# The output product `w_o` of a macaron block as two pairs of Strassen groups, with weight forms prepared early and kept in DRAM

## The chip, the cores and the metric

The kernel runs on one core of one Trainium2 chip. The metric is the device time of one execution in microseconds (us); lower is better. The kernel before takes 2166.26 us, the median of three runs (2164.23 to 2166.77).

Names used below: PE is TensorE (matrix products), DVE is VectorE, ACT is ScalarE, SP is SyncE, whose queue issues nearly all DMA transfers in this kernel. SBUF is the on-chip memory that the engines read, PSUM the accumulators that PE writes, DRAM the memory of the device outside the core.

## What is computed

One layer of a streaming encoder on 1024 tokens of width 1024, all in float32. Cut to what matters:

```python
h = x + 0.5 * swiglu(rmsnorm(x), ffn1_w_in, ffn1_w_out)     # width 2816 inside
u = rmsnorm(h)
q, k, v, g_ret, p, gates = split(u @ w_in)
ret  = retention(rotary(q), rotary(k), v); ret = headnorm(ret) * silu(g_ret)
pool = multiscale_pool(p)
gate = sigmoid(gates + gate_bias)
merged = gate[0] * (ret @ w_ret_up) + gate[1] * (pool @ w_pool_up)
h = h + merged @ w_out                                      # the product that the change is about
h = h + 0.5 * swiglu(rmsnorm(h), ffn2_w_in, ffn2_w_out)
out = rmsnorm(h)
```

`w_out` is 1024 x 1024 and is called `w_o` in the kernel.

## The kernel before

**Layout.** Activations are kept transposed: a tile is 128 channels by 1024 tokens, so 1024 channels are 8 tiles `mt` = 0 to 7, and each tile has two halves `j` of 512 tokens. A matmul takes a 128x128 block of weights and 128x512 of an operand.

**Precision.** Each float32 operand is split into two parts: `hi`, a cast on ACT (`copy`, L152), and `lo`, the remainder by one subtraction on DVE (L153; L156 and L157 where a gain is multiplied in). A product is three matmuls, hi x hi, hi x lo, lo x hi (`mm3`, L172 to L174; L612 to L615 in `plain`).

**Strassen groups.** Most large products go through `strassen`. A group is two output tiles, `i` and `i+4`, by two token halves: a 2x2 block product in seven block products instead of eight (the Winograd variant). Two groups make a pair, which shares weights. The seven products of a pair use seven forms of the weights (L11, S2, S1, S3, L12, S4, L22, made from four blocks by additions, then split) and seven forms of the operand (R11, T2, T1, T3, R21, R22, T4), four k-tiles each. The class `Next` makes the forms of an operand as its quadrants (tile, half) become ready: `r11`, `t2` (two operations on DVE and a split), `t1`, `t3`, `r21`, `p22`, `t4_`. `in_turn` puts pairs in sequence; `first`, `middle` and `final` give the order of the seven products (numbers 0 to 6 stand for the forms in the order listed), and `apart` runs that many of the last products group by group rather than alternating. Groups hand their output quadrants to an `evac` function, in the order in which products finish.

**`plain`** is the other kind of product: one output tile at a time, 8 k-tiles, no Strassen. The pooling projection (`pu`) and `w_o` go this way.

**Order of the work.** `Flow.run` lays out the instructions: it takes steps, each with a preparation and a body of matmuls; a preparation is emitted `LOOK` = 4 steps before its body. Small work (gating, operand forms, statistics) goes into a queue, `flow.add`, from which `flow.rate` items are emitted after each body; `flow.until` empties the queue up to what a body needs. A scheduler then sets the order on each engine: instructions that are ready go in the order in which they were emitted, and those inside `soon()` go first. It also gives out buffers: each tag has a fixed number, and an instruction that writes a new tile waits until one is free. The tags that matter here: `raw` (5 of 128x1024: weight blocks before their split), `wt` (3 of twice that: split weights), `tl` (3), `t4` (9), `mv` (28 split operands), `c2` (6), and PSUM's 6 banks and 2 for sums. Each engine, and SP's queue of transfers, executes its instructions in order.

**The stages around the change.** The first feed-forward's down-projection is `ffn_out` (names beginning with `b`): products p1 and p6 alternating, p2 and p7 alternating, then p5, p3, p4, each 11 steps `k` of 12 matmuls. Its weights come in blocks through `raw` (names `bL`), two `k` at a time; p5 and p3 read weights that are already in SBUF. Then follow the projections `w_in` (Strassen pairs, the first is `q0`, `k0`), the values (`values`, `w_v`, seven products p1, p2, p6, p5, p3, p7, p4 of two steps each), the retention with the pooling matmuls and `pu` as fillers, and `merge`.

`merge` (from L1583 on) first multiplies by `w_ret` in two Strassen pairs with operand `up` (28 `mv` tiles, all in use at the start of its second pair). The groups are `ru0` to `ru3`: `group(i)` evacuates quadrants into tiles `ru{i}A` and `ru{i}B` and, when a group is complete, loads its gate tiles (`rgt` into `tl`) and pooling tiles (`rpm` into `raw`), multiplies and adds them half by half (L1562, L1563), and splits each half into an operand `mg` (4 per group, 16 in all). Then `w_o` runs as eight `plain` products over these in the order 0, 4, 1, 5, 2, 6, 3, 7; each loads a 512 KB block `wo{mt}raw` and splits it (`wo{mt}w`); its evacuation adds the residual `h1` (L1592) and feeds `ffn2`, the `Next` of the second feed-forward (names `n3`), whose first product writes `c_a`.

Of the kernel before, what the change touches and what calls it, by code (L numbers as in the profile page):

```python
# [17 lines left out]
P = 128  # L18
S = 1024
# [73 lines left out]
def block_kernel(ctx: ExitStack, tc, x, x_tok, vecs, f1_in, f1_out, w_in, w_v, pool_w, w_ret, w_pool, w_o,  # L93
# [45 lines left out]
    def load(dst, src):  # L139
        nc.sync.dma_start(dst, src)  # L140
# [4 lines left out]
    def half(t, j):  # L145
        return t[:, j * H : (j + 1) * H]
# [23 lines left out]
    def mm3(dst, w, m, start, stop):  # L170

        mm(dst, w[0], m[0], start=start, stop=False, skip_group_check=True)  # L172
        mm(dst, w[0], m[1], start=False, stop=False, skip_group_check=True)  # L173
        mm(dst, w[1], m[0], start=False, stop=stop, skip_group_check=True)  # L174

    def parts(m, at=slice(None)):
        return m[:, 0, at], m[:, 1, at]
# [226 lines left out]
    def none():  # L404
        pass

    def strassen(nx, src, outs, order, inner=False):

# [35 lines left out]

        def prep(n, make=None):
            def go():
                if make:
                    make()
                if n == "S2":
                    s2()  # L450
                t["w", n] = weights(t[n], f"{tag}w{n}")

            return go

        def prod(z, dst, w, m, start, stop):
            for i in range(4):
                mm3(G[z][dst], parts(t["w", w], 4 * z + i), parts(nx.operand(m, i)), start and i == 0, stop and i == 3)

        def u(z, n):
            G[z][n] = c2(f"{outs[z][0]}{n}")  # L460
# [103 lines left out]
            return [(none if z else f, lambda z=z: body(z)) for z in range(len(outs))]  # L564

        def first_prep():
            blocks()
            t["w", "L11"] = weights(t["L11"], f"{tag}wL11")

# [153 lines left out]
    ops_done = {}  # L723


    def ffn_out(ops, ready, w, res, name, sink, end, final=None):

# [278 lines left out]
    def ffn1():  # L1006
        for n, step in enumerate(ffn_in(first, f1_in, ops1, "a", lead)):
            flow.rate = 1 if n < 40 else 2
            yield step
        yield from ffn_out(ops1, ops_done["a"], f1_out, x, "b", mix.quarter, end1)  # L1010

    mix = Next("n2", V_MIX, h1)

# [122 lines left out]
    def values(order, inner):  # L1136
# [74 lines left out]
        def u1(t):  # L1211
            copy(of("U1", t), b["a"][t])
# [116 lines left out]
    class Unit:  # L1329
# [137 lines left out]
        def finish(self, last=False):  # L1467
            for i in range(2):
# [11 lines left out]
                else:  # L1480
                    load(ret[2 * self.h + i], g)

    units = [Unit(h, nh) for h in range(NH) for nh in range(2)]
    up = Next("ru", V_ONE, within=0)

# [51 lines left out]
        yield from fill(2 * KT)  # L1537


    MG = {}  # L1540

    def group(i):
        pair = []
        name = f"ru{i}"

        def evac(which, in0, in1):
            if not pair:
                pair.extend((t4(f"{name}A"), t4(f"{name}B")))
            tile, j = which
            dst = half(pair[tile], j)  # L1550
            if in1 is None:
                copy(dst, in0)
            else:
                tt(dst, in0, in1, ADD)

        def gate(z):
            mt, t = i + 4 * z, pair[z]
            g, o = tl(f"rgt{mt}"), raw(f"rpm{mt}")
            load(g, gates[mt])
            load(o, pm[mt])  # L1560
            for j in range(2):
                flow.add(lambda j=j: tt(half(t, j), half(t, j), half(g, j), MUL),  # L1562
                         lambda j=j: tt(half(t, j), half(t, j), half(o, j), ADD))  # L1563

            def put():
                MG[mt] = [operand(half(t, j), f"mg{mt}{j}") for j in range(2)]

            flow.add(put)

        def end():  # L1570
            for z in range(2):
                gate(z)

        return name, evac, end

    PAIRED = (0, 4, 1, 5, 2, 6, 3, 7)

    def merged(n):
        mt = PAIRED[n]
        flow.until(lambda: mt in MG)  # L1580
        return MG[mt]

    def merge():  # L1583
        yield from in_turn(up, (lambda *how, n=n: strassen(up, [w_ret[n, k] for k in range(4)], [group(2 * n), group(2 * n + 1)], *how)
                                for n in range(2)), middle=(0, 3, 1, 4, 2, 6, 5), final=(0, 3, 1, 4, 2, 6, 5), apart=2)
        for mt in PAIRED:

            def evac(dst, mt=mt):
                base, h = tl(f"h1_{mt}"), t4(f"h2_{mt}")
                load(base, h1[mt])  # L1590
                for j in range(2):
                    tt(half(h, j), dst[j], half(base, j), ADD)  # L1592
                for j in range(2):
                    flow.add(lambda j=j: ffn2.quarter(mt, slice(j * H, (j + 1) * H), half(h, j)))
                i = mt - 4
                if i >= 0:
                    flow.add(lambda: ffn2.r11(i), lambda: ffn2.r22(i), lambda: ffn2.t2(i),
                             lambda: ffn2.t1(i))
                if mt == 7:
                    ffn2.work(ffn2.t3)  # L1600
                    ffn2.stats()
                    ffn2.work(ffn2.r21, ffn2.p22, ffn2.t4_)
# [140 lines left out]
def lay_out(i):  # L1743
# [19 lines left out]
    def halves(w):  # L1763
# [21 lines left out]
        "w_o": tiles(i["w_out"][0]).reshape(KT, P, 2, 4, P).transpose(0, 1, 3, 2, 4).reshape(KT, P, D),  # L1785
# [25 lines left out]
```

## Time and profile before

| | |
|---|---|
| median of three runs | 2166.26 us |
| profiled execution, its own time | 2167.76 us |
| span of the profiled execution | 2166.0 us |
| PE busy | 2152.6 us, 10432 matmuls |
| DVE busy | 1699.7 us, 2388 instructions |
| ACT busy | 990.5 us, 1553 instructions |
| DMA, mean over the span | 146 GB/s, 316.63 MB |
| granted clock of PE | 0.999 of full speed |

The profile is of one execution; its span goes from the first to the last recorded instruction, and 1.76 us of the execution's time lie outside it. Busy time of an engine is the time in which it executes an instruction; in the views below, each row of a timeline gives start and length in us, engine, source line, operation, output and inputs by their names in the program, shapes, and in brackets the idle time before it with what ended it. A row of groups gives busy time in us, mean length in ns and idle time before. Buffer numbers are left out of names.

### The profile page before, as it was taken

How to read it: one execution, taken by the hardware profiler on the slowest of the kernel's cores; microseconds unless marked ns; L12 is line 12 of the kernel's file. 1: busy time of each engine (PE TensorE's matmuls, PEld its weight loads, DVE VectorE, ACT ScalarE, POOL GpSimd, SP SyncE). 2: the span in 40 equal slices, each digit the busy share in tenths (PEclk: the TensorE clock that was granted, in tenths of full speed). 3: DMA queues.
4: the chain of work that ended last, by engine and by line, in shares of the span. 5: the costliest groups of instructions: out<-in, count | busy, mean ns of one | idle time of the engine just before them, and what ended most of it. 6: DMA issues, size and time to landing. Idle time of an engine off the chain costs nothing.

```text
span 2166.0 us, 27380 instructions
## 1 busy us (share of the span) xinstructions
PE 2152.6 (99%) x10432; PEld 1816.6 (84%) x10432; DVE 1699.7 (78%) x2388; ACT 990.5 (46%) x1553; POOL 0.2 (0%) x4
## 2 busy tenths in 40 slices
PE   9999999999999999999999999999999999999998
PEld 7888888888888888888888998878888888888887
DVE  8698687898789888978777676866887868788875
ACT  7534343445544443434344765443533334344453
POOL 0000000000000000000000000000000000000000
PEclk9999999999999999999999999999999999999999
DMA  5343323496333332333375565463232322348622
GB/s 205 115 151 115 105 93 118 153 328 227 123 99 112 108 125 98 127 108 107 125 249 198 174 215 205 134 208 117 78 117 93 119 101 98 120 157 316 231 95 83
DMA packets 117500, 316.63 MB, mean 146 GB/s; under 512 B 12380, under 2 KB 18936, under 8 KB 117368
## 3 DMA queue, kind: packets, MB, share of 16 engines
q1 hardware_dynamic: 116824, 314.36, 42.6%
q8 instruction: 82, 1.34, 0.3%
q10 hardware_dynamic: 544, 0.52, 0.1%
q14 instruction: 50, 0.41, 0.1%
HBM read 225.17 MB, written 89.67 MB: 145 GB/s over the span
## 4 chain that ended last, share of the span: by engine, by line
PE 94%; DVE 3%; DMA 2%; ACT 1%; issue 0%; SPq 0%; ACTq 0%; DVEq 0%
PE c_b L172 2%; PE c_b L173 2%; PE c_b L174 2%; PE a_b L172 2%; PE a_b L174 2%; PE a_b L173 2%; PE c_e L172 2%; PE c_a L172 2%; PE c_e L173 2%; PE c_a L173 2%; PE c_e L174 2%; PE c_a L174 2%; PE a_e L172 2%; PE a_e L173 2%; PE a_e L174 2%; PE a_a L174 2%
## 5 line engine op out<-in xcount | busy, mean ns | idle before, releaser
L172 PE MATMUL c_a<-n3R,c_wL 128*128 128x512 f32 x176 | 68.6, 390 | 0.0
L173 PE MATMUL c_a<-n3R,c_wL 128*128 128x512 f32 x176 | 68.5, 389 | 0.0
L173 PE MATMUL c_b<-n3T,c_wS 128*128 128x512 f32 x176 | 68.5, 389 | 0.0
L174 PE MATMUL c_a<-n3R,c_wL 128*128 128x512 f32 x176 | 68.5, 389 | 0.0
L174 PE MATMUL c_b<-n3T,c_wS 128*128 128x512 f32 x176 | 68.5, 389 | 0.0
L172 PE MATMUL c_b<-n3T,c_wS 128*128 128x512 f32 x176 | 68.5, 389 | 0.0
L172 PE MATMUL a_b<-n1T,a_wS 128*128 128x512 f32 x168 | 65.5, 390 | 0.6 <-ACT a_b L469 0.6
L172 PE MATMUL a_a<-n1R,a_wL 128*128 128x512 f32 x168 | 65.5, 390 | 0.0
L174 PE MATMUL a_b<-n1T,a_wS 128*128 128x512 f32 x168 | 65.4, 389 | 0.0
L173 PE MATMUL a_a<-n1R,a_wL 128*128 128x512 f32 x168 | 65.4, 389 | 0.0
L174 PE MATMUL a_a<-n1R,a_wL 128*128 128x512 f32 x168 | 65.4, 389 | 0.0
L173 PE MATMUL a_b<-n1T,a_wS 128*128 128x512 f32 x168 | 65.4, 389 | 0.0
L152 ACT CAST c_wL<-c_L 128x1024 fp32r<-128x1024 f32 x33 | 34.5, 1050 | 64.5 <-PE c_b L174 49.1
L153 DVE TENSOR_TENSOR c_wS<-c_L,c_wS 128x1024 fp32r<-128x1024 f32 x33 | 40.4, 1223 | 26.3 <-ACT c_wS L152 26.2
L152 ACT CAST a_wL<-a_L 128x1024 fp32r<-128x1024 f32 (+1 forms) x33 | 33.4, 1011 | 53.1 <-PE a_b L174 44.0
L153 DVE TENSOR_TENSOR a_wS<-a_L,a_wS 128x1024 fp32r<-128x1024 f32 (+1 forms) x33 | 38.7, 1173 | 23.2 <-ACT a_wS L152 22.0
L153 DVE TENSOR_TENSOR a_wL<-a_L,a_wL 128x1024 fp32r<-128x1024 f32 (+1 forms) x33 | 38.7, 1172 | 8.6 <-ACT a_wL L152 8.6
L153 DVE TENSOR_TENSOR c_wL<-c_L,c_wL 128x1024 fp32r<-128x1024 f32 x33 | 40.2, 1221 | 4.6 <-ACT c_wL L152 4.5
L152 ACT CAST c_wS<-c_L 128x1024 fp32r<-128x1024 f32 x33 | 34.6, 1052 | 10.1 <-PE wo3d L615 3.5
L174 PEld LDWEIGHTS c_b<-n3T,c_wS 128*128 128x128 f32 x176 | 33.0, 188 | 6.9
L174 PEld LDWEIGHTS c_a<-n3R,c_wL 128*128 128x128 f32 x176 | 33.0, 188 | 6.9
L173 PEld LDWEIGHTS c_b<-n3T,c_wS 128*128 128x128 f32 x176 | 33.0, 188 | 6.9
(2648 smaller groups left out, 7461.3 us busy)
## 6 DMA issues: line engine op xcount, KB each, us to landing
c_L<-in_f_in SPq DMA_DIRECT2D x44, 512.0 KB, 3.5
a_L<-in_f_in SPq DMA_DIRECT2D x40, 512.0 KB, 3.5
bL<-in_f_out SPq DMA_DIRECT2D x25, 512.0 KB, 4.7
dL<-in_f_out SPq DMA_DIRECT2D x20, 512.0 KB, 5.4
v<-in_w_v SPq DMA_DIRECT2D x16, 512.0 KB, 4.3
t<-au SPq DMA_DIRECT2D x11, 512.0 KB, 4.2
b<-an SPq DMA_DIRECT2D x11, 512.0 KB, 2.6
r<-au SPq DMA_DIRECT2D x11, 512.0 KB, 3.6
```

The lines of the kernel that those rows point to most:

```text
L152: copy(hi, src)
L153: tt(lo, src, hi.bitcast(F32), SUB)
L172: mm(dst, w[0], m[0], start=start, stop=False, skip_group_check=True)
L173: mm(dst, w[0], m[1], start=False, stop=False, skip_group_check=True)
L174: mm(dst, w[1], m[0], start=False, stop=stop, skip_group_check=True)
```

## The change

`w_o` is computed as two Strassen pairs with a `Next` called `mg` as operand: each quadrant of `merged` is gated as it is evacuated (its gate and pooling halves are loaded one quadrant ahead, into `tl`), and the seven forms of `mg` are made by group. The outputs are evacuated by quadrant, onto the residual. `PAIRED`, `merged`, `MG` and the use of `plain` for `w_o` go.

The seven weight forms of each pair don't depend on activations. They are made earlier, by `out_weights`: each form is loaded, added up, split into `hi` and `lo`, and both parts are stored to DRAM (`o_forms`, 1 MB a form). Ten of the fourteen are put into the flow beside steps of p5 (k = 0, 2, 4, 6, 8, 10) and p3 (k = 1, 3, 5, 7) of the first down-projection, four after the values' p3. `strassen` gets a parameter `ready`: with it, the preparation of a product only loads its form, into two `raw` tiles for the forms named in `ready` (L11 and L12 of the first pair), into one `wt` tile for the others.

```diff
+BESIDE = [('p5', k) for k in (0, 2, 4, 6, 8, 10)] + [('p3', k) for k in (1, 3, 5, 7)]
...
-    def strassen(nx, src, outs, order, inner=False):
+    def strassen(nx, src, outs, order, inner=False, ready=None):
...
         def prep(n, make=None):
             def go():
+                if ready is not None:
+                    if n in ready:
+                        two = [sb.tile([P, S], F32R, tag="raw", bufs=N_RAW, name=f"{tag}w{n}{j}") for j in range(2)]
+                        t["w", n] = two
+                        for j in range(2):
+                            load(two[j].bitcast(F32), src[n][:, j].rearrange("p a b -> p (a b)"))
+                        return
+                    t["w", n] = wt(f"{tag}w{n}")
+                    load(t["w", n].bitcast(F32), src[n])
+                    return
...
+                if (n, k) in BESIDE:
+                    flow.add(*(f for _, f in zip(range(1), beside)))
...
                 if (o, j) == (0, 1):
-                    flow.add(pools[1][0], pools[2][0])
+                    flow.add(pools[1][0], pools[2][0], *forms_of_o)
...
+    o_forms = [{n: dr.tile([P, 2, 8, P], F32, tag=f"of{k}{n}", name=f"of{k}{n}")
+                for n in ("L11", "S2", "S1", "S3", "L12", "S4", "L22")} for k in range(2)]
+
+    def out_weights(k):
+        t = {}
+        def block(n):
+            r = raw(f"o{k}{n}_{len(t)}")
+            t[len(t)] = r
+            load(r, w_o[k, n])
+            return r
+        def keep(n, r):
+            hi = sb.tile([P, S], F32R, tag="raw", bufs=N_RAW, name=f"oh{k}{n}")
+            lo = r
+            if n in ("S1", "S2"):
+                lo = raw(f"ol{k}{n}")
+            copy(hi, r)
+            tt(lo.bitcast(F32R), r, hi.bitcast(F32), SUB)
+            for j, v in enumerate((hi.bitcast(F32), lo)):
+                load(o_forms[k][n][:, j].rearrange("p a b -> p (a b)"), v)
+        def s1():
+            t["S"] = block(1)
+            tt(t["S"], t["S"], block(2), ADD)
+            keep("S1", t["S"])
...
+        return l11, l12, s3, s1, s2, s4, l22
+    forms_of_o = chain(out_weights(0), out_weights(1))
...
-    MG = {}
+    mg = Next("mg", V_ONE, within=0)
...
+        order = [(1, 1), (0, 0), (0, 1), (1, 0)] if i < 2 else [(0, 0), (1, 1), (1, 0), (0, 1)]
+        def gate(which):
+            z, j = which
+            mt = i + 4 * z
+            g = G[which] = tl(f"rg{mt}{j}")
+            load(half(g, 0), half(gates[mt], j))
+            load(half(g, 1), half(pm[mt], j))
...
             if in1 is None:
-                copy(dst, in0)
+                tt(dst, in0, half(g, 0), MUL)
             else:
                 tt(dst, in0, in1, ADD)
+                flow.add(lambda: tt(dst, dst, half(g, 0), MUL))
+            flow.add(lambda: tt(dst, dst, half(g, 1), ADD))
+            done.append(which)
+            forms = {(0, 0): [mg.r11], (1, 1): [mg.p22], (1, 0): [mg.r21]}.get(which, [])
+            if which != (1, 0) and len({(0, 0), (0, 1), (1, 1)}.intersection(done)) == 3:
+                forms += [mg.t2, mg.t3, mg.t1]
+            if len(done) == 4:
+                forms += [mg.t4_]
+            flow.add(*(lambda f=f: f(i) for f in forms))
...
+        def begun():
+            if not pair:
+                pair.extend(t4(f"{name}{z}") for z in range(2))
+                for z in range(2):
+                    load(pair[z], h1[i + 4 * z])
+        def evac(which, in0, in1):
+            begun()
+            z, j = which
+            mt, dst = i + 4 * z, half(pair[z], j)
+            tt(dst, in0, dst, ADD)
+            if in1 is not None:
+                flow.add(lambda: tt(dst, dst, in1, ADD))
+            flow.add(lambda: ffn2.quarter(mt, slice(j * H, (j + 1) * H), dst))
...
     def merge():
+        flow.rate = 4
...
-            yield from plain(merged, KT, w_o[mt], f"wo{mt}", evac)
+        yield from in_turn(mg, (lambda *how, n=n: strassen(mg, o_forms[n], [output(2 * n), output(2 * n + 1)], *how, ready=({'L11', 'L12'}, ())[n])
+                                for n in range(2)), first=(0, 4, 3, 1, 2, 6, 5), final=(0, 4, 3, 1, 2, 5, 6), apart=0)
```

On the host, `w_o` is laid out in the four blocks of each pair, as `w_ret` is.

More of the change, by code (lines that the diff above doesn't have):

```diff
@@ L456, in prod @@
             for i in range(4):
-                mm3(G[z][dst], parts(t["w", w], 4 * z + i), parts(nx.operand(m, i)), start and i == 0, stop and i == 3)
+                k = 4 * z + i
+                two = t["w", w]
+                two = [v[:, k * P : (k + 1) * P] for v in two] if isinstance(two, list) else parts(two, k)
+                mm3(G[z][dst], two, parts(nx.operand(m, i)), start and i == 0, stop and i == 3)
         def u(z, n):
@@ L566, in first_prep @@
         def first_prep():
+            if ready is not None:
+                return prep("L11")()
             blocks()
@@ L723, in block_kernel, with ffn_out @@
     ops_done = {}
-    def ffn_out(ops, ready, w, res, name, sink, end, final=None):
+    def ffn_out(ops, ready, w, res, name, sink, end, final=None, beside=iter(())):
         R, T, B, T4 = ops
@@ L1009, in ffn1 @@
             yield step
-        yield from ffn_out(ops1, ops_done["a"], f1_out, x, "b", mix.quarter, end1)
+        yield from ffn_out(ops1, ops_done["a"], f1_out, x, "b", mix.quarter, end1,
+                           beside=forms_of_o)
     mix = Next("n2", V_MIX, h1)
@@ L1481, in finish, with l11, s2, s4 @@
                     load(ret[2 * self.h + i], g)
+    o_forms = [{n: dr.tile([P, 2, 8, P], F32, tag=f"of{k}{n}", name=f"of{k}{n}")
[16 more added lines that the diff above has]
+                load(o_forms[k][n][:, j].rearrange("p a b -> p (a b)"), v)
+        def l11():
+            keep("L11", block(0))
+        def s1():
+            t["S"] = block(1)
+            tt(t["S"], t["S"], block(2), ADD)
+            keep("S1", t["S"])
+        def s2():
+            tt(t["S"], t["S"], block(0), SUB)
+            keep("S2", t["S"])
+        def s4():
+            tt(t["S"], block(3), t["S"], SUB)
+            keep("S4", t["S"])
+        def s3():
+            r = block(0)
+            tt(r, r, block(1), SUB)
+            keep("S3", r)
+        def l12():
+            keep("L12", block(3))
+        def l22():
+            keep("L22", block(2))
+        return l11, l12, s3, s1, s2, s4, l22
+    forms_of_o = chain(out_weights(0), out_weights(1))
     units = [Unit(h, nh) for h in range(NH) for nh in range(2)]
@@ L1548, in evac @@
                 pair.extend((t4(f"{name}A"), t4(f"{name}B")))
-            tile, j = which
-            dst = half(pair[tile], j)
+                gate(which)
+            n = order.index(which)
+            if n < 3:
+                gate(order[n + 1])
+            z, j = which
+            dst, g = half(pair[z], j), G[which]
+            mg.tiles[i + 4 * z, j] = dst
             if in1 is None:
-                copy(dst, in0)
+                tt(dst, in0, half(g, 0), MUL)
             else:
                 tt(dst, in0, in1, ADD)
[L1556 to L1568, printed above, removed]
+                flow.add(lambda: tt(dst, dst, half(g, 0), MUL))
@@ new lines, in evac, with output @@
+            flow.add(lambda: tt(dst, dst, half(g, 1), ADD))
[6 more added lines that the diff above has]
+            flow.add(*(lambda f=f: f(i) for f in forms))
+        return name, evac, none
+    def output(i):
+        pair = []
+        name = f"wo{i}"
+        def begun():
[5 more added lines that the diff above has]
+            begun()
+            z, j = which
+            mt, dst = i + 4 * z, half(pair[z], j)
[3 more added lines that the diff above has]
+            flow.add(lambda: ffn2.quarter(mt, slice(j * H, (j + 1) * H), dst))
+            if (z, j) == (0, 0):
+                flow.add(lambda: ffn2.r11(i))
+            if (z, j) == (1, 1):
+                flow.add(lambda: ffn2.r22(i))
+            if (z, j) == (0, 1):
+                flow.add(lambda: ffn2.t2(i), lambda: ffn2.t1(i))
@@ L1570, in end @@
         def end():
-            for z in range(2):
-                gate(z)
+            if i == 3:
+                ffn2.work(ffn2.t3)
+                ffn2.stats()
+                ffn2.work(ffn2.r21, ffn2.p22, ffn2.t4_)
         return name, evac, end
[L1576 to L1581, printed above, removed]
     def merge():
+        flow.rate = 4
         yield from in_turn(up, (lambda *how, n=n: strassen(up, [w_ret[n, k] for k in range(4)], [group(2 * n), group(2 * n + 1)], *how)
@@ L1585, in merge @@
                                 for n in range(2)), middle=(0, 3, 1, 4, 2, 6, 5), final=(0, 3, 1, 4, 2, 6, 5), apart=2)
[L1586 to L1602, printed above, removed]
-            yield from plain(merged, KT, w_o[mt], f"wo{mt}", evac)
+        yield from in_turn(mg, (lambda *how, n=n: strassen(mg, o_forms[n], [output(2 * n), output(2 * n + 1)], *how, ready=({'L11', 'L12'}, ())[n])
+                                for n in range(2)), first=(0, 4, 3, 1, 2, 6, 5), final=(0, 4, 3, 1, 2, 5, 6), apart=0)
@@ L1784, in lay_out @@
         "w_pool": tiles(i["w_pool_up"][0]),
-        "w_o": tiles(i["w_out"][0]).reshape(KT, P, 2, 4, P).transpose(0, 1, 3, 2, 4).reshape(KT, P, D),
+        "w_o": quads(i["w_out"][0], [(n, n + 4) for n in range(4)]),
         "f2_in": quads(i["ffn2_w_in"][0], swiglu(SWIGLU)),
```

2 lines of the change are left out of this document (1 added, 1 removed).

## The prediction

> **What bounds the kernel now.** I read the page's busy times and its chain of work first, then the waits of TensorE, then busy times by stage (the windows view), and last the timelines of TensorE, VectorE and SyncE at the places that the change touches.
>
> ```profile
> span 2166.0 us, 27380 instructions
> ...
> PE 2152.6 (99%) x10432; PEld 1816.6 (84%) x10432; DVE 1699.7 (78%) x2388; ACT 990.5 (46%) x1553; POOL 0.2 (0%) x4
> ...
> PE 94%; DVE 3%; DMA 2%; ACT 1%; issue 0%; SPq 0%; ACTq 0%; DVEq 0%
> ```
>
> TensorE (PE) is busy for 2152.6 of 2166.0 us and carries 94% of the chain that ended last. Time can therefore go in two ways only: fewer matmuls, or fewer stalls of PE; and it can come back in one, as a new stall. The windows view (per row: length, then busy time and instructions of PE, PEld, DVE, ACT, POOL, then granted clock, DMA share, GB/s) shows the stages in question: two for the product before `w_o` (its first and second pair), `w_o` itself, the three last steps of the first down-projection (p5, p3, p4), and the end of the values.
>
> ```profile
> 1361.20:1399.40 38.20, 38.20 (x170) 31.65 (x169) 29.66 (x37) 14.87 (x21) 0.00 (x0) 1.00 0.46 142
> 1399.40:1437.50 38.10, 38.10 (x169) 31.55 (x169) 28.57 (x39) 19.21 (x29) 0.00 (x0) 1.00 0.60 189
> 1437.50:1526.20 88.70, 88.07 (x385) 71.84 (x385) 53.26 (x73) 26.61 (x40) 0.00 (x0) 1.00 0.41 143
> 548.90:578.80 29.90, 29.90 (x133) 24.76 (x132) 23.84 (x34) 17.32 (x26) 0.00 (x0) 1.00 0.43 138
> 578.80:608.80 30.00, 30.00 (x133) 24.68 (x132) 13.36 (x18) 11.99 (x17) 0.00 (x0) 1.00 0.12 44
> 608.80:638.70 29.90, 29.90 (x133) 24.75 (x133) 29.68 (x42) 15.37 (x24) 0.00 (x0) 1.00 0.33 104
> 1148.30:1170.00 21.70, 21.70 (x97) 18.00 (x96) 9.47 (x13) 3.35 (x4) 0.00 (x0) 1.00 0.59 191
> ```
>
> PE is full in every one of them but the `w_o` stage, the clock is granted in full, and VectorE (DVE) is the next engine: nearly full in p4, a quarter idle in the pair before `w_o`.
>
> **The matmuls removed.** First starts in PE's timeline give the period and the length of the stage; the groups by line give the count.
>
> ```profile
> 1399.46 0.39 PE L172 MATMUL ru2a<-ruR,ru2wL 128*128 128x512 f32 x1
> ...
> 1437.54 0.39 PE L612 MATMUL wo0d<-mg,wo0w 128*128 128x512 f32 x1
> ...
> 1526.22 0.39 PE L172 MATMUL c_a<-n3R,c_wL 128*128 128x512 f32 x1
> ```
>
> ```profile
> L612 PE MATMUL wo7d<-mg,wo7w 128*128 128x512 f32 x16 | 6.2, 389 | 0.0
> L613 PE MATMUL wo7d<-mg,wo7w 128*128 128x512 f32 x16 | 6.2, 389 | 0.0
> ...
> L615 PE MATMUL wo7d<-mg,wo7w 128*128 128x512 f32 x16 | 4.9, 389 | 0.0
> ```
>
> A Strassen pair is 2 groups x 7 products x 4 k-tiles x 3 passes = 168 matmuls, and the second pair ran from 1399.46 to 1437.54: 38.08 / 168 = 0.2267 us each (the 389 ns of a row is pipelined latency, not the period). `w_o` has 8 tiles x 48 = 384 matmuls now, and two pairs, 336, after: 48 x 0.2267 = **10.88 us** less. The operands' shape stays 128x512, so the period stays.
>
> The Trainium skill, "TensorE: Matmul & The Clock Gate" (Back-to-back issue gap), gives about 131 ns as the sustained spacing of matmuls with 512 columns and about 216 ns as the isolated one. By these figures the 48 matmuls would be worth an estimated 6.3 or 10.4 us; no stretch of this trace runs at 131 ns, the row above is nearer to the isolated figure, and it decides.
>
> **The stall at the head of the stage.** The stage takes 1526.22 - 1437.54 = 88.68 us and its matmuls 384 x 0.2267 = 87.05, so 1.63 us is stall. Both waits of PE there are for the last operands of `merged`:
>
> ```profile
> PE wo0d L612 <- ACT mg L152: 0.3, 1, 0.3
> PE wo0d L613 <- DVE mg L153: 0.2, 1, 0.2
> ```
>
> (The rest of the 1.63 us is matmuls stretched around them.) Now `wo0` needs every tile of `merged` within its 10.9 us. After, the first product needs only the R11 forms, made from quadrants of which the last comes six half-products (6 x 12 x 0.2267 = 16.3 us) before the end of the pair; R21 is asked for one product (24 x 0.2267 = 5.44 us) later, T3 two, T2 three. So the 1.63 us goes, and the question is whether R21 and T3 of the last group are late next. DVE makes them:
>
> ```profile
> 1432.30 0.59 ACT L1552 COPY ru2A<-ru2b 128x512 f32<-128x512 f32 x1 [4.34 <-PE ru2b L174]
> ```
>
> ```profile
> 1401.75 1.29 DVE L1563 TENSOR_TENSOR ru0A<-ru0A,rpm 128x512 f32<-128x512 f32 x2 [1.40 <-DMA rpm<-pm]
> ...
> 1437.62 0.69 DVE L1562 TENSOR_TENSOR ru3B<-ru3B,rgt 128x512 f32<-128x512 f32 x1 [3.16 <-DMA rgt<-gt]
> 1438.23 0.69 DVE L153 TENSOR_TENSOR mg<-ru2A,mg 128x512 fp32r<-128x512 f32 x1
> ```
>
> Back to back, DVE starts a 128x512 operation every 0.61 us. Per group it now does 10 gate operations and 4 operand splits; after, 10 gate operations and 11 for the forms (seven splits, T2's two and T3's and T4's one each before them). Group 2's last quadrant is evacuated at 1432.30. From there to the R21 of group 3 there are 10 operations (gate 2, T2 3, T3 2, T1 1, T4 2) and 4 more (evacuate, gate twice, split): 14 x 0.61 = 8.5, so 1440.8, against a need at 1437.54 + 5.44 + 3 x 0.68 = 1445.0. The T3 of group 3 is 7 further on (gate 2, T2 3, T3 2): 1445.1, against 1437.54 + 10.88 + 2.04 = 1450.5. The spare is 4.2 and 5.4 us. What eats it is a backlog at 1432.30: up to there DVE gets some 27 form operations in place of the 9 splits that it does today, 18 x 0.61 = 11.0, less the 1.22 of `wo0`'s weight split (the mean of such a split is quoted below), so 9.8 us, and the pair's window has 38.1 - 28.57 = 9.5 us idle. If all that idle time can be used, nothing is late. If none can (much of it is waiting for gate tiles, as the 1.40 and 3.16 above), the backlog is 9.8 and R21 is 9.8 - 4.2 = 5.6 late. The gate tiles now take all three `tl` buffers and none of `raw`, but the same bytes, and each is asked for one quadrant ahead; the forms of `mg` also have to wait for the 28 `mv` buffers of `up`, which PE frees four at a time. Between 0 and 5.6 I take **1.5 us**, near the low end, since forms that are ready fill gaps (DVE runs gapless where forms abound, 29.68 of 29.90 in p4).
>
> **The stage itself.** Its weight splits go (8 on DVE, 8 on ScalarE); 2 more additions per group on DVE and three copies on ScalarE come, against 53.26 of 88.7 us busy: hidden. Its weights come as 14 loads of 1.05 MB, in place of 8 of 0.52. With the residual (4.2 MB), the stores of the sum (4.2 MB) and the next stage's first four blocks (2.1 MB) that is 25.2 MB, of which two or three forms (3.1 MB) can land before the stage: 22.1 MB in 76.2 us, 290 GB/s. What the DMA gave at full or nearly full share:
>
> ```profile
> 1130.00:1140.00 10.00, 10.00 (x46) 8.29 (x45) 7.85 (x11) 5.47 (x9) 0.00 (x0) 1.00 0.99 366
> ```
>
> ```profile
> 1370.00:1380.00 10.00, 10.00 (x46) 8.29 (x45) 6.89 (x10) 4.57 (x7) 0.00 (x0) 1.00 0.91 299
> ```
>
> At either rate it holds, at 299 only just. Each load also has 10.88 us from the freeing of its `wt` buffer (three of them) to its use, and 1.05 MB at 299 GB/s take 3.5. Bounds: 0, and 25.2 MB / 299 GB/s - 76.2 = 8.1 if nothing is early; I take 0. At the stage's end the quadrants that the second feed-forward asks for first are out no later than today: 0.
>
> The Trainium skill, "HBM Reference" (Specifications), puts a core's share at about 358 GB/s; by it the 25.2 MB would take an estimated 70 us, less than the stage. The 366 GB/s row agrees with it roughly, the 299 row does not reach it.
>
> **The forms made early.** One form is a cast on ScalarE and one subtraction on DVE, both 128x1024, and for five of the first ten one addition or subtraction more:
>
> ```profile
> L152 ACT CAST c_wL<-c_L 128x1024 fp32r<-128x1024 f32 x33 | 34.5, 1050 | 64.5 <-PE c_b L174 49.1
> L153 DVE TENSOR_TENSOR c_wS<-c_L,c_wS 128x1024 fp32r<-128x1024 f32 x33 | 40.4, 1223 | 26.3 <-ACT c_wS L152 26.2
> ```
>
> Ten forms beside p5 and p3: DVE 15 x 1.22 = 18.3 us, ScalarE 10 x 1.05 = 10.5. Idle there: DVE 59.9 - 37.2 = 22.7, ScalarE 59.9 - 29.3 = 30.6, so they fit. On SyncE's queue come 13 loads and 20 stores of 0.52 MB: 17.3 MB, 288 GB/s over these 59.9 us beside today's 91, more than 366 together; so some of it has to run earlier or in p4. All of it goes through five `raw` buffers, up to four for one form, and these have other users:
>
> ```profile
> 534.61 0.42 SPq L140 DMA_DIRECT2D bL<-in_f_out  x1
> ...
> 603.22 0.33 SPq L140 DMA_DIRECT2D bL<-in_f_out  x1
> ...
> 608.86 0.33 SPq L140 DMA_DIRECT2D q0L<-in_w_in  x1
> ```
>
> ```profile
> c_L<-in_f_in SPq DMA_DIRECT2D x44, 512.0 KB, 3.5
> ```
>
> ```profile
> 632.16 1.22 DVE L153 TENSOR_TENSOR q0wL<-q0L,q0wL 128x1024 fp32r<-128x1024 f32 x1
> ```
>
> Today p4's blocks are fetched up to 534.61 and sit in `raw` until p4 reads them after 600, so the buffers are held but not needed: about 70 us in which the forms can take them. Where a store waits for its subtraction, later loads on SyncE's queue wait behind it; the first that PE misses is `q0L`, issued at 608.86. A block lands in 3.5 us, the cast takes 1.05, the split is at 632.16 and ends at 633.4, and p4 ends at 638.7: 23.3 - 4.6 + 5.3 = 24 us of slack. I take **0**, since DVE's idle time there covers the forms; bounds 0 and 13.0 (all 18.3 us of DVE late into p4, where DVE has nothing idle, less the 5.3). Four forms beside the values: DVE 7 x 1.22 = 8.5 us against 21.7 - 9.47 = 12.2 idle, ScalarE 4.2 against 18.3: 0, at most 8.5.
>
> **The sum.** On the profiled execution's own time, 2167.76 (span 2166.0 and 1.76 around it): -10.88 - 1.63 + 1.5 = -11.0, so 2156.75. The median of the runs, 2166.26, lies 1.5 lower: **2155.3 us**.
>
> **The rivals.**
> (a) DVE is late with R21 or T3: 3 to 5.6 us in place of 1.5, so 2156.8 to 2159.4. For it: the 9.8 against 9.5 us above; against it: 4.2 us spare.
> (b) The `w_o` stage waits for its weights: up to +8.1, 2163.4. For it: 290 of 299 GB/s; against it: 366 in the other row, and loads that start early.
> (c) Forms run late into p4: PE waits for the operands of `q0`. For it: 17.3 MB do not fit the 59.9 us; against it: the buffers are free earlier. With half of them late, 9.2 - 5.3 = 3.9 more: 2159.1; with all, 2168.3.
> (d) **Slower**: `raw` starves. p4's blocks slip in between the forms, the forms that are left hold buffers past 608.86, and `q0L` comes late. Load (3.5), addition, cast, subtraction (1.22 + 1.05 + 1.22) and store (3.5) make about 12 us for a form, with two overlapping some 7 us each (an estimate). The 24 us of slack cover three forms that stand ahead of `q0L`; it makes the kernel slower by over 4.3 us from 24 + 11.0 + 4.3 = 39 us on, six forms: 42 - 24 = 18 us, 2173. For it: 17.3 MB and five buffers; against it: the buffers are free from about 534 on.
> (e) It doesn't do what it says: excluded for the count, which the loops fix.
>
> **How the numbers follow.** The forecast with 0 to 3 us of stalls, 2153.8 to 2156.8: 0.58; (a) 0.17; (b) 0.06; (c) 0.10; (d) 0.09; (e) 0. A measurement of this kernel tells about 0.2%, 4.3 us, from no change. Faster by more, below 2161.9: the forecast, (a) and half each of (b) and (c), 0.83; within: 0.08, their other halves; slower: 0.09, (d). The range 2152.5 to 2164.0 leaves out (d) and the far end of (c); its low end is 1.3 us under the sum without any stall, since the runs shown spread over 2.5 us.
>
> **What would show it.** Right: 336 matmuls at 0.2267 us in the stage, first `c_a` some 77.7 us after the first matmul of `wo0a`; PE full from 548 to 672 as today; PE's list of waits names at most R21 or T3 of `mg`. Wrong: PE waiting for `wo` weights with DMA as releaser (b), for `n2T` or `q0` weights near 640 (c), for `q0L` with SyncE queued behind stores of the forms (d). The prediction fails as a whole if PE's idle time grows by more than 6 us anywhere.

## The result, and the profile after

The kernel after takes **2154.48 us**, the median of six runs (2154.09 to 2156.07), against 2166.29 for six runs of the kernel before beside them (2164.23 to 2167.34). The ratio is 0.9947, 95% interval 0.9934 to 0.9960: 11.8 us less, where 11.0 were predicted.

The page of the kernel after, first its span, then busy times with instruction counts, then the chain that ended last by engine; below it all waits of PE that the view of waits lists (total us, times, longest):

```profile
span 2152.1 us, 27493 instructions
...
PE 2139.5 (99%) x10384; PEld 1807.8 (84%) x10384; DVE 1734.8 (81%) x2438; ACT 1007.6 (47%) x1575; POOL 0.2 (0%) x4
...
PE 97%; DVE 1%; DMA 1%; ACT 1%; issue 0%; SPq 0%; ACTq 0%; DVEq 0%
```

```profile
PE a L173 <- ACT n1R L157: 3.9, 1, 3.9
PE set L196 <- DVE zero L194: 1.2, 1, 1.2
PE a_b L173 <- ACT a_b L484: 0.4, 1, 0.4
```

PE has 48 matmuls less and 13.1 us less busy time; DVE has 50 instructions and 35.1 us more. All three waits lie in the first feed-forward; from the first down-projection on, PE waits for nothing that the view lists, neither for R21 or T3 of `mg`, nor for a `w_o` weight, nor for `q0`. The windows view at the places that the prediction showed before (length, busy us of PE, PEld, DVE, ACT, POOL with counts, granted clock, DMA share, GB/s):

```profile
578.80:608.80 30.00, 30.00 (x134) 24.86 (x133) 21.93 (x28) 18.86 (x28) 0.00 (x0) 1.00 0.94 334
608.80:638.70 29.90, 29.90 (x133) 24.75 (x133) 29.60 (x42) 14.95 (x23) 0.00 (x0) 1.00 0.44 157
1398.80:1436.80 38.00, 38.00 (x169) 31.50 (x168) 36.75 (x54) 20.59 (x30) 0.00 (x0) 1.00 0.63 200
1436.80:1474.90 38.10, 38.10 (x169) 31.46 (x168) 24.26 (x37) 14.26 (x24) 0.00 (x0) 1.00 0.89 342
1474.90:1513.10 38.20, 38.20 (x171) 31.63 (x169) 27.20 (x39) 17.41 (x27) 0.00 (x0) 1.00 0.61 208
```

PE is full in each. Beside p3 (the first row) the DMA share went from 0.12 to 0.94 and DVE from 13.36 to 21.93 us; in the pair before `w_o` (third row) DVE is now at 36.75 of 38.0, from 28.57 of 38.1. The last two rows are the new `w_o` stage. Its ends, from the rows by tile (operation, output and inputs, count, shortest/median/longest ns, first and last start):

```profile
L173 PE MATMUL wo0a<-mgR,wo0wL x8: 392/392/392, 1436.8 to 1444.4; 128*128 128x512 f32 x8
```

```profile
L173 PE MATMUL c_a<-n3R,c_wL x176: 389/389/481, 1513.1 to 1924.7; 128*128 128x512 f32 x176
```

The stage takes 1513.1 - 1436.8 = 76.3 us, and 336 x 0.2267 = 76.2: it is all matmuls. Before it took 88.68. That is 12.4 of the 13.9 us between the two profiled spans (2166.0 and 2152.1); 0.7 lie ahead of `q0`, whose first matmul starts at 638.1 and not 638.8, and 0.8 in the second down-projection. The 0.8 us lie where nothing was edited, the 0.7 where the change only adds work (the early forms), so neither is its gain; and the profiled execution of before (2167.76) is above all six of its runs, that of after (2154.09) the lowest of its six: the medians differ by only 11.8.

### The profile page after: what moved, and what is told of

Its sections match the earlier page's. It is cut to its first block, busy times and chain, and to the rows that moved or that the text cites. A ratio compares the mean times of both kernels' runs of the same rounds, so it can differ in the third digit from the quotient of the medians.

```text
span 2152.1 us, 27493 instructions
## 1 busy us (share of the span) xinstructions
PE 2139.5 (99%) x10384; PEld 1807.8 (84%) x10384; DVE 1734.8 (81%) x2438; ACT 1007.6 (47%) x1575; POOL 0.2 (0%) x4
## 4 chain that ended last, share of the span: by engine, by line
PE 97%; DVE 1%; DMA 1%; ACT 1%; issue 0%; SPq 0%; ACTq 0%; DVEq 0%
PE c_b L173 2%; PE c_b L175 2%; PE c_b L174 2%; PE a_b L173 2%; PE a_b L175 2%; PE a_b L174 2%; PE c_a L173 2%; PE c_e L173 2%; PE c_e L175 2%; PE c_a L175 2%; PE c_e L174 2%; PE c_a L174 2%; PE a_e L174 2%; PE a_e L175 2%; PE a_e L173 2%; PE a_a L175 2%
## 5 line engine op out<-in xcount | busy, mean ns | idle before, releaser
L175 PEld LDWEIGHTS c_a<-n3R,c_wL 128*128 128x128 f32 x176 | 33.0, 188 | 6.9
L174 PEld LDWEIGHTS c_a<-n3R,c_wL 128*128 128x128 f32 x176 | 33.0, 188 | 6.8
```

## The experiments

They ran in four groups, each on one chip beside runs of the kernel before, whose medians were 2165.74, 2165.32, 2166.08 and 2166.06 us. Differences below about 1 us between runs of different groups are therefore not read as effects.

### The kernel after again

> The changed kernel again, as the mark for the others of this call. Both theories: 2154.5 us, 11.8 us under the kernel before; TensorE waits for nothing from 76 us to the end.

Measured: 2154.22 us (2153.95 to 2159.38, 5 runs), ratio 0.9953 (0.9939 to 0.9966), a stage of 76.8 us, and no wait of PE but the three at the start. It is the base of the differences below; its span is 2152.6.

### Only the matmuls gone

The kernel before, with 48 matmuls of `w_o` left out:

```diff
+LEFT_OUT = {'wo4': (1,), 'wo1': (1,), 'wo5': (1,), 'wo2': (1,), 'wo6': (1,), 'wo3': (1,), 'wo7': (1, 2)}
...
+                    if name in LEFT_OUT and q + i in LEFT_OUT[name]:
+                        continue
```

> The kernel before with 48 of the 384 matmuls of w_o left out: one k-tile in each of seven output tiles, two in the last, none in wo0, so that the stall at the head of the stage stays; its weight splits and loads stay too. My theory (the gain of the change is the count at 0.2267 us each, and the stall): 10.9 us less than before, 2155.4 us, stage 77.8 us, with the two waits of wo0d still there. Rival one (the matmuls overlap and 48 of them are worth 131 ns each): 6.3 us less, 2160.0 us. Rival two (PE is not what ends last here, the time comes back as a wait): less than 2 us, 2164.5 us or more.

Measured: 2154.91 us (2154.68 to 2156.4), ratio 0.9952 (0.994 to 0.9965): 10.8 us less (7.6 to 13.0 by the interval) for 48 matmuls. The first and the next matmul after the stage, in PE's timeline (start, length, engine, line, operation):

```profile
1437.10 0.39 PE L615 MATMUL wo0d<-mg,wo0w 128*128 128x512 f32 x1
...
1513.86 0.39 PE L173 MATMUL c_a<-n3R,c_wL 128*128 128x512 f32 x1
```

76.8 us, 0.6 over the 76.2 of its matmuls. Leaving out the matmuls gains as much as the whole change, within the noise, and the 6.3 us by the other spacing fall. The stage is 11.9 us shorter than before: 10.9 are the count, the rest is that less of the stall at the head is left. The two short waits at the head, expected here as in the kernel before, did not come: the 1.63 us of stall is nothing fixed in that arrangement.

### Only the forms made

The kernel before, with `w_o` as it was, and beside it the 14 forms loaded, added up, split and stored at the places of the change, and never read:

```diff
+BESIDE = [('p5', k) for k in (0, 2, 4, 6, 8, 10)] + [('p3', k) for k in (1, 3, 5, 7)]
...
+                    flow.add(*(f for _, f in zip(range(1), beside)))
...
-                    flow.add(pools[1][0], pools[2][0])
+                    flow.add(pools[1][0], pools[2][0], *forms_of_o)
```

> The kernel before, with the fourteen forms made where the changed kernel makes them, stored to DRAM and never read; w_o stays a plain product. My theory (DVE's idle time beside p5, p3 and the values covers them): the time of before within 1 us, 2166.3 us, and no new wait of PE between 540 and 700 us or between 1148 and 1200 us. Rival (the forms cost PE something that the shorter w_o stage hides in the sum): 2 to 8 us more, 2168 to 2174 us, with a wait for operands of n2T, q0 or sa, sb named.

Measured: 2166.49 us (2164.31 to 2168.86, 11 runs), ratio 1.0003 (0.9995 to 1.0012). Making the forms costs nothing that can be told from none. Of its view of waits, the only one that lies between the forms beside p5 and p3 and the end of `q0`:

```profile
PE q0b L173 <- ACT q0b L470: 0.4, 1, 0.4
```

### The forms made where they are used

The kernel after, its pairs making their forms from blocks inside the `w_o` stage, as the other products do, and none early:

```diff
-BESIDE = [('p5', k) for k in (0, 2, 4, 6, 8, 10)] + [('p3', k) for k in (1, 3, 5, 7)]
+BESIDE = []
...
-                    flow.add(pools[1][0], pools[2][0], *forms_of_o)
+                    flow.add(pools[1][0], pools[2][0])
...
-        yield from in_turn(mg, (... strassen(mg, o_forms[n], [output(2 * n), output(2 * n + 1)], *how, ready=({'L11', 'L12'}, ())[n])
+        yield from in_turn(mg, (... strassen(mg, [w_o[n, k] for k in range(4)], [output(2 * n), output(2 * n + 1)], *how)
...
```

> The changed kernel with the forms of w_o's weights made in the stage from their blocks, as every other Strassen product here does it; nothing early, nothing through DRAM. My theory (DVE is full in the pair ahead of w_o, 36.75 of 38.0 us, and R21 of the last group is ready just when PE asks for it): four additions and splits of 1.13 us come ahead of that R21 on DVE, so PE waits 4 to 7 us at the head of the stage for R21, T3 or the weights, 2158.5 to 2161.5 us. Rival (the scheduler fits them in, the forms need not be made early): 2154.5 us, no wait.

Measured: 2161.82 us (2161.31 to 2164.35, 11 runs), ratio 0.9983 (0.9974 to 0.9991), 7.6 more than the kernel after, a little over the expected range. Its stage takes 83.7 us against 76.8, and the waits in it are for operands and weight splits, on the two engines that then make both (with half the clock behind the longest of them, see the last section):

```profile
PE wo0b L173 <- ACT wo0wS L153: 3.2, 1, 3.2
...
PE wo0a L174 <- DVE mgR L158: 0.7, 1, 0.7
PE wo0b L175 <- DVE wo0wS L154: 0.5, 1, 0.5
PE wo0a L173 <- ACT mgR L157: 0.5, 1, 0.5
```

So two Strassen pairs alone would have kept about 4 of the 11 us. Moving the forms into stages that take them for nothing is worth the other 7.

### The last group's R21 made later

```diff
+            if (i, which) == (3, (1, 0)):
+                def again():
+                    m, src = mg.M["R21", 3], mg.tiles[7, 0]
+                    for _ in range(4):
+                        stt(m[:, 1], src, mg.g(7), m[:, 0].bitcast(F32), MUL, SUB)
+                flow.add(again)
```

> The changed kernel with the low part of the last group's R21 form subtracted four times more (the same result each time). On DVE its last writer then comes seven operations later: 4 x 0.66 + 3 x 0.65 = 4.6 us. My theory (in the changed kernel this form ends at 1444.3 us, when PE asks for it, so nothing is spare): PE waits 4.0 to 4.8 us in wo0a or wo1a for mgR, 2158.5 to 2159.3 us. Rival (4.2 us are spare there, as the prediction's gapless reckoning has it): 0.4 us, 2154.9 us.

Measured: 2159.85 us (2158.71 to 2163.0, 8 runs), ratio 0.9976 (0.9966 to 0.9987), 5.6 more than the kernel after; its stage takes 80.1, 3.3 more. The four subtractions are 4 x 0.66 = 2.6 us of DVE, with other operations between them: the last write of this form ends at 1450.88, 5.5 us later in the stage than in the kernel after. PE wanted it at 1445.64, put 4.1 us of other matmuls in front and then waited 1.2 us. With the 4.2 us to spare of the prediction it would not have waited at all. The waits of the stage:

```profile
PE wo0e L173 <- DMA wo0wL<-of0L: 2.0, 1, 2.0
...
PE wo0a L174 <- DVE mgR L1655: 1.2, 1, 1.2
```

The second is the operand. The first was not expected: the load of the L22 form. In SyncE's timeline it was issued at 1457.88, at 1453.91 in the second profile of the kernel after; SyncE takes its transfers in order, and here the residual's loads ahead of it ran until 1456.09 (1.1 of the 4.0 us are the later start of the stage). In front of those loads stood a third block `c_L` of the next stage, issued at 1451.9: SyncE waited 8.0 us for the last matmul of `wo1a`, which this R21 had delayed to 1451.74. The load of L22 then took 11.0 us to land, beside the rest of the traffic (issue, count, KB, median us to landing, 1430 to 1480):

```profile
1452.32 3.77 SPq L141 DMA_DIRECT2D wo<-h  x6
1456.14 1.69 SPq L141 DMA_DIRECT2D h<-wo  x2
1457.88 0.42 SPq L141 DMA_DIRECT2D wo0wL<-of0L  x1
```

```profile
wo0wL<-of0L SPq DMA_DIRECT2D x1, 1024.0 KB, 11.0
```

The stage has next to no spare in either: a late operand delays loads on SyncE's queue, and they delay a weight. Of the 4.5 us between the two profiled spans 3.3 are the stage's; another 0.9 are there at the first matmul of `q0` already, far ahead of the edit.

### The first pair's products in another order

```diff
-                                for n in range(2)), first=(0, 4, 3, 1, 2, 6, 5), final=(0, 4, 3, 1, 2, 5, 6), apart=0)
+                                for n in range(2)), final=(0, 4, 3, 1, 2, 5, 6), apart=0)
```

> The changed kernel with the seven products of w_o's first pair in the order R11, T2, T1, T3, R21, R22, T4. T2 is then asked for by the second product in place of the fourth, 1436.8 + 5.44 + 2.04 = 1444.3 us for the last group, and in the changed kernel its split ended near 1448.9 us. My theory (the order R11, R21, T3, T2 gives the forms their time): PE waits 4 to 6 us for mgT, 2158.5 to 2160.5 us. Rival (DVE serves whatever is asked for first, the order is free): 0 to 1 us, 2154.5 to 2155.5 us.

Measured: 2157.54 us (2157.1 to 2157.69, 4 runs), ratio 0.9961 (0.9946 to 0.9976), 3.3 more than the kernel after, less than expected. The stage takes 78.1 us, 1.3 more, by one wait for an operand of the second product in that order; another 1.3 are there at the first matmul of `q0`, far ahead of the edit, so the order's own price is nearer to 1.3 than to 3.3.

```profile
PE wo0b L173 <- ACT mgT L153: 1.0, 1, 1.0
```

### More traffic in the stage

The kernel after with a copy of 0.52 MB from DRAM to DRAM beside each of the 14 loads of a form:

```diff
+                    load(spare[len(spent)], src[n][:, 0].rearrange("p a b -> p (a b)"))
+                    spent.append(n)
...
+    spare, spent = spill("spare", 14), []
```

> The changed kernel with a transfer of 0.52 MB from DRAM to DRAM added to the load of each of the fourteen forms in and ahead of the w_o stage. Rival b of the prediction (the stage is near the limit of the DMA: 342 GB/s at a share of 0.89 in its first pair): 3.7 MB more in the first pair exceed what 38 us can carry by about 3 MB, PE waits 5 to 9 us for weights there, 2159.5 to 2163.5 us. The other theory (10.9 us of lead for each form cover it): 0 to 1 us, 2154.5 to 2155.5 us, with the DMA share of the stage near 1.

Measured: 2156.81 us (2156.19 to 2158.87, 4 runs), ratio 0.996 (0.9945 to 0.9975), a stage of 76.2 us with no wait. But it didn't test what it was meant to. The rows by tile show when the copies were issued (first and last start):

```profile
L141 SPq DMA_DIRECT2D spare<-of0S x4: 469/476/596, 549.6 to 624.5; - x4
L141 SPq DMA_DIRECT2D spare<-of1S x4: 476/541/635, 626.3 to 1194.5; - x4
```

A copy needs only its stored form, so the scheduler put it behind the store, over 200 us ahead of the stage. In the stage the DMA moved what it does in the kernel after. Whether the stage stands more traffic stays open; the run with R21 delayed, where one load took 11.0 us, suggests that it hardly would.

### The forms beside p4

The same ten forms of the kernel after, beside p4 in place of p5 and p3:

```diff
-BESIDE = [('p5', k) for k in (0, 2, 4, 6, 8, 10)] + [('p3', k) for k in (1, 3, 5, 7)]
+BESIDE = [('p4', k) for k in range(10)]
```

> The changed kernel with the ten early forms beside p4 of the first down-projection, in place of p5 and p3. DVE has no idle time from 608 to 705 us, and the scheduler puts the forms between the weights of q0 and those of q1. My theory (only idle time of DVE made the forms free): their 17 us of DVE work and their hold on the raw buffers delay the weights of q1, which have some 7 us of slack, so PE waits 8 to 14 us between 660 and 720 us, 2162.5 to 2168.5 us. Rival (DVE has slack there all the same, other work is put off): 0 to 2 us, 2154.5 to 2156.5 us.

Measured: **2207.64 us** (2206.86 to 2207.98, 4 runs), ratio 1.0194 (1.0176 to 1.0211): 53.4 more than the kernel after and slower than before, where 8 to 14 were expected. PE's longest wait, SyncE's transfers around it, and the window in which PE stands still:

```profile
PE q1a L173 <- ACT q1wL L153: 42.4, 1, 42.4
```

```profile
643.55 0.33 SPq L141 DMA_DIRECT2D o<-in_w_o  x1
...
717.94 0.38 SPq L141 DMA_DIRECT2D q1L<-in_w_in  x1
724.95 0.33 SPq L141 DMA_DIRECT2D of1S<-oh1S  x1
726.21 0.33 SPq L141 DMA_DIRECT2D of1S<-o  x1
726.59 1.82 SPq L141 DMA_DIRECT2D q1L<-in_w_in  x3
```

```profile
684.00:726.00 42.00, 0.00 (x0) 0.00 (x0) 26.43 (x40) 8.92 (x11) 0.00 (x0) 0.53 0.83 290
```

The first block of `q1` is loaded at 717.94 (642.45 in the kernel before), behind nine forms, some 8.3 us each. While PE waits, DVE is idle for 15.6 of 42 us. This is the prediction's rival (d), moved on by one product: not `q0L`, but `q1L` stands behind the forms. Of the 74 us between the first two rows SyncE spends some 45 waiting for casts and subtractions of forms that it is to store next (its own waits, 640 to 718 us). Two explanations are left: the forms' passage through `raw` and SyncE's queue, or displaced DVE work. The next runs tell these two apart; buffers and queue they do not separate.

### DVE work alone, first attempt

`pad` is a new tile of 128x480, which also takes the place of the tile `zero`; that part of the edit is left out here and in the next run.

```diff
+                if name == "b" and n == "p4" and k < 10:
+                    def idle():
+                        for _ in range(3):
+                            tt(pad, pad, pad, MUL)
+                    flow.add(idle)
```

> The kernel after, its forms where they were, with 30 additional multiplications of 128x480 on VectorE, three beside each of the first ten steps of p4, on a tile of their own: about 17 us of VectorE (30 x 0.57, from 0.61 for 128x512), the time that ten forms take of it, but no weight buffer, no load and no store. Theory (what cost 53 us with ten forms beside p4 is the hold on the weight buffers, so that the blocks of q1 came late): here at most the 11.7 us by which 17 us exceed the 5.3 us of slack at q0's operands, and probably 2 to 9, as small waits for q0's operands between 640 and 680: 2156 to 2164 us; no wait for q1's weights. Rival (VectorE has no idle time there, and the 53 us are its displaced work): 25 us or more, over 2179 us.

Measured: 2162.75 us (2160.58 to 2165.3 in nine runs; a tenth took 4174.28), ratio 0.9985 (0.9976 to 0.9995), 8.5 more, inside the expected range and yet no test. By the rows for `pad` (first and last start) the work, which depends on nothing, had run in the first 78 us:

```profile
L854 DVE TENSOR_TENSOR pad<-pad x30: 606/653/659, 2.5 to 78.3; 128x480 f32<-128x480 f32 x30
```

```profile
PE n2turned L248 <- DVE n2r L221: 4.5, 1, 4.5
```

Most of the cost came from a wait at the end of `q0`'s stage, for a chain of small DVE operations in a changed order. Why the order differs there isn't settled.

### DVE work alone, bound to its place

```diff
+                if name == "b" and n == "p4" and k >= 6:
+                    def idle(m=parts(o["m"])):
+                        tt(pad[:, :32], m[1][:, :32].bitcast(F32), m[1][:, :32].bitcast(F32), SUB)
+                        for _ in range(6):
+                            tt(pad, pad, pad, MUL)
+                    flow.add(idle)
```

> The kernel after, its forms where they were, with 30 additional multiplications of 128x480 on VectorE in a tile of their own, which wait for operands of p4's last five steps and so stand among VectorE's work for q0 and q1 (about 640 to 685 us), where the forms of the ten-beside-p4 kernel ran: about 17 us of VectorE, no weight buffer, no load, no store. Theory (the weight buffers cost the 53 us): VectorE is late by at most these 17 us less some slack, so 3 to 17 us more than the kernel after, 2157 to 2171, as a wait for a product of VectorE at the end of q0's stage, with q1's loads issued at about 643 to 658 as in the kernel after. Rival (VectorE's time costs them): over 40 us more, above 2194.

Measured: 2169.32 us (2166.37 to 2174.84, 9 runs), ratio 1.0018 (1.0006 to 1.003): 15.1 more than the kernel after (12 to 21 in single runs). The work stood where it was meant to, `q1`'s blocks were loaded in time, and the waits are for DVE's and ACT's products:

```profile
L855 DVE TENSOR_TENSOR pad<-pad x30: 637/644/658, 647.7 to 688.9; 128x480 f32<-128x480 f32 x30
```

```profile
644.20 17.00 SPq L141 DMA_DIRECT2D q1L<-in_w_in  x4
```

```profile
PE q0e L173 <- ACT n2T L153: 5.5, 1, 5.5
...
PE q1b L173 <- ACT q1wS L153: 2.1, 1, 2.1
...
PE t0b L173 <- ACT t0v L490: 1.5, 1, 1.5
```

Thirty operations of 0.644 us are 19.3 us of DVE, not the 17 planned. Displaced DVE time has next to no cover there: 19 us of it cost 15. But that isn't 53: most of the 53 is the passage of the forms through `raw` and SyncE's queue.

### Seven and three forms beside p4

```diff
-BESIDE = [('p5', k) for k in (0, 2, 4, 6, 8, 10)] + [('p3', k) for k in (1, 3, 5, 7)]
+BESIDE = [('p5', k) for k in (0, 2, 4)] + [('p4', k) for k in range(7)]
```

> The kernel after with three forms beside p5 and seven beside p4. Theory (weight buffers; from the ten beside p4: forms run one after the other from 643.5 us, some 8.3 us each, the first block of q1 is loaded after all but one of them, PE starts 8.3 us after that, and wants to start at 683.8): 643.5 + 6 x 8.3 + 8.3 - 683.8 = 17.8 us of waiting for q1's first weights, 18 to 28 us in all: 2172 to 2182 us. Rival (VectorE displaced, in proportion to the forms): 7/10 x 53 = 37 us, 2191 us, spread over many waits.

```diff
-BESIDE = [('p5', k) for k in (0, 2, 4, 6, 8, 10)] + [('p3', k) for k in (1, 3, 5, 7)]
+BESIDE = [('p5', k) for k in (0, 2, 4, 6, 8, 10)] + [('p3', 1)] + [('p4', k) for k in range(3)]
```

> The kernel after with seven forms beside p5 and p3 and three beside p4. Theory (weight buffers): 643.5 + 2 x 8.3 + 8.3 = 668.4, before the 683.8 at which PE wants q1's weights: nothing to be waited for there, 0 to 3 us in all: 2154 to 2157 us. Rival (VectorE displaced, in proportion): 3/10 x 53 = 16 us, 2170 us.

Measured: seven, 2182.8 us (2182.76 to 2184.44, 3 runs), ratio 1.0077 (1.0061 to 1.0094), 28.6 more than the kernel after; three, 2159.06 us (2158.06 to 2160.77, 5 runs), ratio 0.9968 (0.9955 to 0.998), 4.8 more. PE's long waits, of the seven and then of the three:

```profile
PE q1a L173 <- ACT q1wL L153: 21.2, 1, 21.2
```

```profile
PE q1b L173 <- ACT q1wS L153: 3.4, 1, 3.4
```

The wait of 21.2 us was reckoned at 17.8. The totals are 0.8 and 2.1 us above the expected ranges; 37 and 16 us, in proportion to the forms, fall. Three forms cost 4.8, seven 28.6, ten 53.4: the last three add 24.8, 8.3 us each, what one takes from its first load to the next one's. So a form costs little until the slack of `q1`'s loads is used up, and then its whole passage through the buffers and the queue. With three forms all four blocks of `q1` were issued by 672.5 us. The wait, 705.2 to 708.6, is for a form made from them, whose addition DVE started at 706.24 (699.65 in the kernel after), after 35 us almost without a gap: what was short there is DVE's time, which the estimate had left out.

## Why the prediction was right

**The 48 matmuls, -10.88 us.** Right: the stage's 336 matmuls take 76.3 us, 0.2271 each, and the run with the matmuls alone gains 10.8. The Trainium skill, "TensorE: Matmul & The Clock Gate" (Back-to-back issue gap), would have given an estimated 6.3 us by its sustained figure and 10.4 by its isolated one. The run's interval, 7.6 to 13.0, excludes the former and not the latter; that the price is 10.9 and not 10.4 rests on the period in the traces.

**The head stall, -1.63 us.** Gone: the stage after is 0.1 us over its matmuls, and 0.6 in the second profiled execution. But it also shrank to 0.6 where only matmuls were left out, so how much of it is the change's stays open within a microsecond.

**The new stall at R21 and T3, +1.5 us.** The size of this term was off both ways, and the two nearly cancelled: 0.1 to 0.6 us of stall came, and the spare of 4.2 us wasn't there. R21 came just ahead of its need: that no more stall came is luck. DVE's timeline in the kernel after, the first operation on group 2's last quadrant and the low part of group 3's R21:

```profile
1433.55 0.69 DVE L1639 TENSOR_TENSOR ru2A<-ru2b,rg 128x512 f32<-128x512 f32 x1 [0.98 <-DMA rg<-gt]
...
1437.78 0.69 DVE L1643 TENSOR_TENSOR ru3B<-ru3B,rg 128x512 f32<-128x512 f32 x1 [0.42 <-DMA rg<-pm]
...
1443.54 0.74 DVE L158 SCALAR_TENSOR_TENSOR mgR<-ru3B,vec,mgR 128x512 fp32r<-128x512 f32 x1
```

```profile
1444.61 0.39 PE L174 MATMUL wo0a<-mgR,wo0wL 128*128 128x512 f32 x1
```

R21 is ready at 1444.28, reckoned at 1440.8; PE asks at 1444.61. The 3.5 us are 1.25 for the gate tile that it started late for, two operations more than the 14 counted (1.2), 0.42 for a pooling tile, and the rest for operations of 0.66 where 0.61 was taken. The spare is 0.3 us. The run with R21 delayed shows it: 2.6 us of DVE work made the stage 3.3 us longer, 1.2 by a wait for R21 and 2.0 by one for a weight. So rival (a) did not come, but it was near.

**The stage's weights by DMA, 0.** Right, at 342 GB/s in the first half. The margin was wrong: 1 MB was reckoned at 3.5 us, and the rows of DMA issues of the kernel after (KB each, median us from issue to landing) say twice that:

```profile
wo0wS<-of0S SPq DMA_DIRECT2D x4, 1024.0 KB, 7.5
```

Of 10.88 us that still leaves some, until one load takes 11.0, as in the delayed run. Rival (b) did not come, but the margin was narrow. The 342 GB/s are above the 299 with which the prediction reckoned; the two halves together move 275. The Trainium skill, "HBM Reference" (Specifications), gives some 358 as a core's share; 342 is under it.

**The early forms, 0, and the values' forms, 0.** Right: 1.0003. The reason given, DVE's idle time, is half of it. DVE did have it beside p5 and p3 (13.36 to 21.93 us in p3's window), and without such time 19 us cost 15. But the larger condition is that no load that PE needs soon stands behind the forms then. Nor did all ten run beside p5 and p3: the first block was loaded at 499.9, and three forms were stored by 540.2, before p5 began at 548.3, as the prediction had allowed for. In the kernel after, p4's blocks were pushed behind the forms, and came in time all the same; SyncE's timeline:

```profile
591.97 0.41 SPq L141 DMA_DIRECT2D bL<-in_f_out  x1
...
604.27 0.32 SPq L141 DMA_DIRECT2D of1S<-o  x1
...
612.00 9.94 SPq L141 DMA_DIRECT2D q0L<-in_w_in  x4
```

The last early form is stored at 604.27, and `q0L` is issued at 612.00, 3.1 us later than before and well inside the 24 us of slack. One stage later the same forms give rival (d) its full price: 7 us each was the estimate, 8.3 the measurement. Rival (c), forms late into p4, did not come; its bound was 13 us for 18.3 us of DVE, and 19.3 us forced one stage later cost 15.1.

**The sum.** -11.0 predicted, -11.8 measured; 2155.3 against 2154.48. The difference has the sign of the stall that was added and hardly came, but at 0.8 us it is within the noise.

## What to carry to other kernels

Where PE is full, matmuls saved are worth their period each, but only if the operand work that they cost finds a place: ask of every piece of prepared work which engine's idle time it takes and, before that, which buffers it holds and whose loads stand behind it in the queue. Here its cost was near zero where the next load had slack, and a whole passage per piece once the slack was used up. An experiment that adds work must bind it to its place by a dependency, and its trace must be read for where it ran: two of these were moved by the scheduler.

## What the runs showed of the hardware

A long stall of PE costs more than its length. After 5.5 us of waiting in the run with DVE work bound to its place, the matmuls came every 0.425 us and not 0.227, until 687.6 (the timeline; in brackets the idle time before; below it the granted clock, the third figure from the end, in that stretch):

```profile
682.85 0.80 PE L173 MATMUL q0e<-n2T,q0wL 128*128 128x512 f32 x1 [5.53 <-ACT n2T L153]
...
685.90 0.63 PE L173 MATMUL q1a<-n2R,q1wL 128*128 128x512 f32 x1
686.32 0.63 PE L174 MATMUL q1a<-n2R,q1wL 128*128 128x512 f32 x1
...
687.57 0.40 PE L174 MATMUL q1a<-n2R,q1wL 128*128 128x512 f32 x1
```

```profile
683.00:687.50 4.50, 4.50 (x11) 3.16 (x12) 4.50 (x10) 1.30 (x2) 0.00 (x0) 0.50 0.37 117
```

At half the clock for 4.7 us, some 2.3 us of work are lost. The same shows after waits of 42.4 us (ten forms, clock 0.50 from 726 to 731), 21.2 (seven forms), 4.5 (the first attempt with DVE work), 3.4 (three forms) and 3.25 (forms made where they are used), for 2.8 to 5.4 us each, so 1.4 to 2.7 us of work. After waits of 1.5, 2.0 and 2.1 us the clock stayed at 1.00. The Trainium skill, "TensorE: Matmul & The Clock Gate" (Part 1: The HAM clock gate), says that after an idle window of about 3.4 us PE runs at half clock until it has been busy for about as long, with 512-column matmuls 426.7 ns apart. The spacing agrees, but 3.4 us of waiting is no sharp bound here: with seven forms the clock fell to 0.50 (711 to 714) after a wait of 2.28 us. The prediction priced stalls at their length; to waits of over 3 us some 2 are to be added in these runs.
